# A convolution's tap matrices split ahead of time and a second channel tile on VectorE in a four-layer encoder kernel

## The chip, the cores and the metric

The kernel runs on one core of one Trainium2 chip. A core has a TensorE for matmuls (PE; its weight loads are shown as PEld), a VectorE (DVE), a ScalarE (ACT), a GpSimd engine (POOL) and a SyncE (SP) that issues most DMAs; ACT and POOL issue some too. Each engine works through its own queue in order; waits between engines are semaphores that a library sets from the data dependences. The metric is the device time of the whole program in microseconds (us). Data lie in SBUF (128 partitions) and PSUM (eight banks of 128 x 512 floats, which TensorE writes).

## The reference

The input is x of 512 tokens by 1024 channels in float32. Four layers follow; each adds a token mixer and then a channel mixer to x:

```python
for i in range(DEPTH):                     # 4
    mixer, j = i % N_MIXERS, i // N_MIXERS
    h = rmsnorm(x, norm1_g[i])
    if mixer == 0:   y = conv_module(h, ...)      # layers 0 and 3
    elif mixer == 1: y = nat_mixer(h, ...)        # layer 1
    else:            y = retention_mixer(h, ...)  # layer 2
    x = x + y
    x = x + conv_ffn(rmsnorm(x, norm2_g[i]), ...)

def conv_module(h, w_in, b_in, dw_w, dw_b, ln_g, ln_b, w_out):
    a, gt = jnp.split(h @ w_in + b_in, 2, axis=-1)
    u = a * jax.nn.sigmoid(gt)
    u = dwconv(u, dw_w, dw_b)              # 31 taps over the tokens, each channel by itself
    u = layernorm(u, ln_g, ln_b)
    return jax.nn.silu(u) @ w_out
```

The change is in the two uses of `conv_module` (layers 0 and 3, j = 0 and 1) and in the channel mixers `conv_ffn` of layers 0, 1 and 2.

## The kernel before

**Precision.** Every float32 operand of a matmul is split in two parts: a high part, cast by ScalarE to the reduced format fp32r, and a low part, the difference, made by VectorE. Three matmuls replace one: high by high, high by low, low by high (`mm3`, L161 to L164, for most; L483 to L485 for the taps). A weight tile (`load_w`, L154 to L159) is loaded on SP into one of two `wraw` buffers, cast into one of three `whi` buffers (L157) and subtracted into one of three `wlo` buffers (L158). `split` (L171 to L173) does the same for other tiles.

**Stages.** `ffn(l, after)` is a channel mixer: 44 up projections `up(n)` of 24 matmuls each, in pairs (value and gate), each pair followed by `mid` on VectorE and ScalarE; then eight output tiles of 66 matmuls. `conv(j, after)` is the convolution module.

**A convolution.** The 1024 channels are eight tiles m of 128. `front(m)` makes the two input projections of a tile (48 matmuls of 128 x 512) and from them u = a * sigmoid(g). Seven tiles take the TensorE path: u is copied by eight small GpSimd DMAs (L435) to `xf`, in which a partition holds a channel and a phase of time, and split into `X`. `taps(m, X, half)` then runs the 31 taps as matmuls against tap matrices, in four units per tile, two per half. A unit is one 128 x 1216 piece of `cdw`: loaded on SP into `raw` (608 KB, five buffers, L473), split into `W` (high and low, three buffers), and used by 2 groups x 5 slots x 3 = 30 small matmuls (64 x 128 or 64 x 112 outputs). A half ends with VectorE adding the bias into `y` (L494), and at set points with `bn_stats` (L502) for the layer norm over channels; the table `BNG` says which units' channels are counted together and after which unit.

Tile 6 (`CD`) takes the VectorE path: `direct` runs its 31 taps as 31 `scalar_tensor_tensor` over 128 x 512 (L446; the last, L454, in two halves that also reorder), `CTAPS` of them in each step of the loop, and at the end four transposes on TensorE (L460) and a copy on ScalarE put the result into `y`. The statistics of the RMS norm are made in between: `stats1` (sums, four transposes, a chain of small VectorE operations to `rstd_col`) and `stats2` (four transposes that broadcast it, L209).

The loop that orders this is L511 to L519: step n emits `front` of the n-th tile of `CORDER` (6, 0, 1, 2, 3, 4, 5, 7), then some direct taps, then the second half of the taps of the tile two back, then the first half of the tile one back. After the last taps, 13 matmuls on old data (L507) fill the time of the layer norm's statistics.

**What sets the order.** Inside the `TileContext` a planner simulates the program, emits instructions to each engine's queue when they are ready in its own clock, with the order in the source as priority, and gives out buffers. `tc.high_priority` (`hp()`) raises a priority; `tc.issue_after(i)` (through `behind(name)`) holds back what is traced in its block until instruction i stands ahead of it on the same engine. A stage's pools may reuse the memory of the stage before, tile by tile. In the first convolution (`early`) the first weights are loaded at the start of the program and some order is written by hand.

## Time and profile before

| | us |
|---|---|
| median of three runs | 2578.81 (2578.18 to 2578.84) |
| the profiled execution, device time | 2577.98 |
| its span in the trace | 2576.2 |
| TensorE busy | 2558.8 |
| VectorE, ScalarE, GpSimd busy | 1652.3, 1050.0, 258.8 |
| bytes moved by DMA | 271.78 MB, 105 GB/s on average |

The stages follow one another: the first convolution until about 205 us, its channel mixer until 590, the neighbourhood attention until 830, the next mixer until 1200, the retention until 1630, the third mixer until 2001.6, the second convolution until 2201, the last mixer until the end. A row of the timeline gives start, duration, engine, line and operation, output and inputs, shape and count; the bracket behind it says how long the engine was idle before it and what ended that. Matmuls are pipelined: their rows overlap, so the distance between starts is their price. A few matmul records are missing from the trace.

### The profile page before, as it was taken

Reading aid. Unit: us, or ns where it says so; the run is one execution under the profiler, and the core shown is the slowest. Engines: PE = TensorE matmul, PEld = TensorE weight load, DVE = VectorE, ACT = ScalarE, POOL = GpSimd, SP = SyncE. Lnnn points to the kernel's source line nnn. Section 1 sums busy time; section 2 is a strip of 40 time slices with the busy share of each in tenths; the row PEclk is TensorE's granted clock in tenths of the full one; section 3 lists DMA queues with packets and bytes.
Section 4 is the critical chain, followed back from the end, with each engine's and each line's share of the span. In section 5 each row is a group of like instructions: output and inputs, shape, how many; then the busy total and the mean of one; then the engine's idle time right before and its main releaser. Section 6 shows DMA issues by size and latency. Waiting matters only on the chain.

```text
span 2576.2 us, 33719 instructions
## 1 busy us (share of the span) xinstructions
PE 2558.8 (99%) x13414; PEld 2120.2 (82%) x13414; DVE 1652.3 (64%) x2673; ACT 1050.0 (41%) x1439; POOL 258.8 (10%) x301
## 2 busy tenths in 40 slices
PE   9999999999999999999999999999999999999999
PEld 7878888889998888888888888888888888788888
DVE  7986777338877777624656566677743787677732
ACT  5554444335556444423333323444432445444421
POOL 1213000003421100000000000100000221100000
PEclk9999999999999999999999999999999999999999
DMA  6724232333332322233222221232333672222232
GB/s 241 234 86 148 90 98 88 95 103 105 97 91 71 101 95 95 90 97 110 74 85 71 84 80 58 98 99 90 97 90 97 206 222 74 90 93 95 92 107 80
DMA packets 80174, 271.78 MB, mean 105 GB/s; under 512 B 10720, under 2 KB 13664, under 8 KB 80016
## 3 DMA queue, kind: packets, MB, share of 16 engines
q1 hardware_dynamic: 73152, 256.32, 30.9%
q0 software_dynamic: 5568, 10.59, 1.7%
q10 hardware_dynamic: 1296, 2.72, 0.3%
q8 instruction: 105, 1.72, 0.3%
q14 instruction: 53, 0.43, 0.1%
HBM read 260.19 MB, written 5.63 MB: 103 GB/s over the span
## 4 chain that ended last, share of the span: by engine, by line
PE 97%; DVE 2%; ACT 0%; issue 0%; DMA 0%; SPq 0%; DVEq 0%; ACTq 0%
PE ps L164 27%; PE ps L163 27%; PE ps L162 27%; PE ps L168 3%; PE ps L169 3%; PE ps L167 3%; PE ps L485 1%; PE ps L484 1%; PE ps L483 1%; PE ps L332 1%; PE ps L333 1%; PE ps L337 1%; PE ps L724 1%; DMA x<-in_xT 0%; PE ps L539 0%
## 5 line engine op out<-in xcount | busy, mean ns | idle before, releaser
L157 ACT CAST wh<-wr 128x1024 fp32r<-128x1024 f32 (+1 forms) x410 | 423.1, 1033 | 1086.1 <-PE ps L163 775.9
L164 PE MATMUL ps<-xh,wl 128*128 128x512 f32 x1856 | 735.4, 397 | 0.1
L163 PE MATMUL ps<-xl,wh 128*128 128x512 f32 x1856 | 734.5, 396 | 0.2 <-DVE xl L232 0.2
L162 PE MATMUL ps<-xh,wh 128*128 128x512 f32 x1856 | 730.4, 394 | 0.4 <-ACT wh L157 0.4
L158 DVE TENSOR_TENSOR wl<-wr,wh 128x1024 fp32r<-128x1024 f32 (+1 forms) x407 | 494.9, 1216 | 334.4 <-ACT wh L157 332.1
L162 PEld LDWEIGHTS ps<-xh,wh 128*128 128x128 f32 x1856 | 348.5, 188 | 85.8 <-ACT wh L157 1.3
L163 PEld LDWEIGHTS ps<-xl,wh 128*128 128x128 f32 x1856 | 348.4, 188 | 85.9 <-DVE xl L232 0.5
L164 PEld LDWEIGHTS ps<-xh,wl 128*128 128x128 f32 x1856 | 348.3, 188 | 81.7 <-DVE wl L158 0.5
L162 PE MATMUL ps<-hh,wh 128*128 128x512 f32 (+1 forms) x726 | 281.6, 388 | 0.5 <-DVE x L362 0.5
L163 PE MATMUL ps<-hl,wh 128*128 128x512 f32 (+1 forms) x726 | 281.5, 388 | 0.0
L164 PE MATMUL ps<-hh,wl 128*128 128x512 f32 (+1 forms) x726 | 281.5, 388 | 0.0
L298 DVE TENSOR_TENSOR t<-ps,rstd_bc 128x512 f32<-128x512 f32 x176 | 120.8, 690 | 159.1 <-PE ps L164 159.1
L250 POOL TENSOR_TENSOR sqacc<-t,sqacc 128x512 f32<-128x512 f32 x49 | 75.1, 1533 | 1253.6 <-ACT t L245 1248.2
L162 PEld LDWEIGHTS ps<-hh,wh 128*128 128x128 f32 x726 | 136.6, 188 | 31.0 <-DVE x L362 0.7
L163 PEld LDWEIGHTS ps<-hl,wh 128*128 128x128 f32 x726 | 136.7, 188 | 30.3
L164 PEld LDWEIGHTS ps<-hh,wl 128*128 128x128 f32 x726 | 136.7, 188 | 30.3
L168 PE MATMUL ps<-wl,xh 128*128 128x256 f32 (+1 forms) x512 | 159.1, 312 | 0.5 <-DVE wl L158 0.5
L169 PE MATMUL ps<-wh,xl 128*128 128x256 f32 (+1 forms) x512 | 159.1, 312 | 0.0
L167 PE MATMUL ps<-wh,xh 128*128 128x256 f32 (+1 forms) x512 | 158.4, 312 | 0.0
L301 ACT ACTIVATE t<-t,par 128x512 f32<-128x512 f32 x176 | 142.5, 814 | 6.0 <-DVE t L298 5.8
L305 DVE SCALAR_TENSOR_TENSOR t<-t,par,t 128x511 f32<-128x511 f32 x176 | 132.0, 750 | 5.5
L303 DVE SCALAR_TENSOR_TENSOR t<-t,par,t 128x511 f32<-128x511 f32 x176 | 130.8, 744 | 0.0
(256 smaller groups left out, 3572.4 us busy)
## 6 DMA issues: line engine op xcount, KB each, us to landing
wr<-in_f_up SPq DMA_DIRECT2D x176, 512.0 KB, 3.4
wraw<-in_cdw SPq DMA_DIRECT2D x56, 608.0 KB, 5.1
wr<-in_f_down SPq DMA_DIRECT2D x64, 448.0 KB, 3.3
wr<-in_f_down SPq DMA_DIRECT2D x32, 512.0 KB, 3.5
wr<-in_cw_in SPq DMA_DIRECT2D x30, 512.0 KB, 3.9
wr<-in_nat_qkv SPq DMA_DIRECT2D x24, 512.0 KB, 3.5
wr<-in_cw_out SPq DMA_DIRECT2D x16, 512.0 KB, 3.9
wr<-in_ret_qk SPq DMA_DIRECT2D x16, 512.0 KB, 3.5
```

The source lines that it names most:

```text
L157: nc.scalar.copy(hi[:, :n], raw[:, :n])
L158: eng.tensor_tensor(lo[:, :n], raw[:, :n], hi[:, :n].bitcast(F32), SUB)
L162: nc.tensor.matmul(o, wh, ah, start=first, stop=False)
L163: nc.tensor.matmul(o, wh, al, start=False, stop=False)
L164: nc.tensor.matmul(o, wl, ah, start=False, stop=last)
L167: nc.tensor.matmul(o, ah, wh, start=first, stop=False)
L168: nc.tensor.matmul(o, ah, wl, start=False, stop=False)
L169: nc.tensor.matmul(o, al, wh, start=False, stop=last)
L298: nc.vector.tensor_tensor(u, ps, rstd_bc, MUL)
L301: nc.scalar.activation(a, u, AF.Identity, bias=pc("fdb", l * 44 + c), scale=pt[:, w + 1:w + 2])
L303: nc.vector.scalar_tensor_tensor(a[:, 1:], u[:, :T - 1], pt[:, w:w + 1], a[:, 1:], MUL, ADD)
L305: nc.vector.scalar_tensor_tensor(a[:, :T - 1], u[:, 1:], pt[:, w + 2:w + 3], a[:, :T - 1], MUL, ADD)
```

## The change

Three things are changed.

1. The tap matrices of the second convolution's remaining 24 units (`UNITS`) are split during the channel mixers of layers 0, 1 and 2: at the odd n from 5 to 35 of each, `split_taps` loads half a unit, splits it and stores both parts to a tile in HBM (`wsp`). 3 x 16 halves are 24 units. The second convolution loads the finished pair (128 x 2 x 1216) straight into `W`, which has five buffers there, and makes no split.
2. In the second convolution tile 5 joins tile 6 on the VectorE path: `CDS` lists the tiles, the order is 6, 5, 0, 1, 2, 3, 4, 7, the direct taps come up to 10 in a step, and the first taps on TensorE start one step later. One group of `bn_stats` is taken at a later unit there.
3. Order, in both convolutions: the direct taps are emitted behind the taps of their step and end a step earlier; the transposes of a direct tile (`direct_out`) are held behind the latest tap matmul. In the first convolution the splits of `W` for a first half are held behind the tile's `X`. In the second the front of a tile is held behind the taps ahead of it. The RMS statistics get the high priority, and some weight loads and matmuls near them are held behind `rstd_col` or the broadcast transposes.

```diff
-BNG = ((0, 16, 16), (16, 28, 24), (28, 30, 30), (30, 31, 31), (31, 32, 32))
+BNG = (((0, 16, 16), (16, 28, 24), (28, 30, 30), (30, 31, 31), (31, 32, 32)),
+       ((0, 16, 16), (16, 28, 30), (28, 30, 30), (30, 31, 31), (31, 32, 32)))
-CORDER = (CD, 0, 1, 2, 3, 4, 5, 7)
-CTAPS = (0, 3, 5, 5, 5, 5, 5, 3, 0, 0)
+CDS = ((6,), (6, 5))
+CORDER = ((6, 0, 1, 2, 3, 4, 5, 7), (6, 5, 0, 1, 2, 3, 4, 7))
+CTAPS = ((0, 4, 5, 5, 6, 6, 5, 0, 0, 0), (0, 5, 10, 10, 10, 9, 9, 9, 0, 0))
+UNITS = [m * 4 + b for m in CORDER[1][2:] for b in range(4)]
...
     def ffn(l, after):
+            sp = st.enter_context(tc.tile_pool(name=nm("sp"), bufs=1, reuse_waits=RW))
+            def split_taps():
+                unit, g = state["units"].pop(0)
+                c = slice(g * GW, (g + 1) * GW)
+                raw = sp.tile([P, GW], F32, tag="raw", name=nm("spr"))
+                nc.sync.dma_start(raw, cdw[1, unit][:, c])
+                w = sp.tile([P, 2, GW], F32R, tag="w", name=nm("spw"))
+                split(raw, w[:, 0], w[:, 1])
+                nc.gpsimd.dma_start(wsp[unit][:, :, c], w.bitcast(F32))
...
                 if n > 1:
                     ups.append(up(n))
+                if n % 2 and 5 <= n <= 35 and l < DEPTH - 1:
+                    split_taps()
...
-                def front(m):
+                def front(m, n):
+                    nd = len(CDS[j])
...
-                        stats1()
-                        stats2(rph)
+                        with hp():
+                            stats1()
+                            stats2(rph)
                     else:
                         for (ps, c) in ((pg, m + 8), (pa, m)):
-                            wh, wl = load_w(cw_in[j, c], D)
+                            pin = m == CORDER[j][1] and c == (m if early else m + 8)
+                            with behind("col") if c == m == CORDER[j][2 if early else 1] else ExitStack():
+                                wh, wl = load_w(cw_in[j, c], D)
                             for k in range(KD):
                                 s = slice(k * P, (k + 1) * P)
-                                mm3(ps, wh[:, s], wl[:, s], xhi[k], xlo[k], k == 0, k == KD - 1)
+                                held = j and c == m + 8 and k == 0 and n > nd + 1
+                                with behind("tap") if held else behind("bc") if pin and k == (6 if early else 1) or early and m + 8 == c == CORDER[j][2] + 8 and k == 0 else ExitStack():
+                                    mm3(ps, wh[:, s], wl[:, s], xhi[k], xlo[k], k == 0, k == KD - 1)
...
+                def direct_out(m):
+                    with behind("tap"):
+                        ps, yr = bank(psb), state["yr"]
                         for r in range(SH):
                             nc.tensor.transpose(ps[:, r * P:(r + 1) * P], yr[:, r * P:(r + 1) * P], ident)
-                        nc.scalar.copy(y[:, :, CD * P:(CD + 1) * P],
-                                       ps.rearrange("p (r c) -> p r c", r=SH))
+                        nc.scalar.copy(y[:, :, m * P:(m + 1) * P], ps.rearrange("p (r c) -> p r c", r=SH))
...
                 def taps(m, X, half):
+                    X, state["xc"], state["xl"] = X
...
-                        raw = dp.tile([P, 2 * GW], F32, tag="wraw", name=nm("wraw"), bufs=5)
-                        if early and m * 4 + b < 5:
-                            after_squares(raw[:, :1])
-                        nc.sync.dma_start(raw, cdw[j, m * 4 + b])
-                        W = dp.tile([P, 2, 2 * GW], F32R, tag="W", name=nm("W"), bufs=3)
-                        with tc.issue_after(state["u"].ins) if early and m * 4 + b < 5 else ExitStack():
-                            split(raw, W[:, 0], W[:, 1])
+                        W = dp.tile([P, 2, 2 * GW], F32R, tag="W", name=nm("W"), bufs=5 if j else 3)
+                        if j:
+                            nc.sync.dma_start(W.bitcast(F32), wsp[m * 4 + b])
+                        else:
+                            raw = dp.tile([P, 2 * GW], F32, tag="wraw", name=nm("wraw"), bufs=5)
+                            if early and m * 4 + b < 5:
+                                after_squares(raw[:, :1])
+                            nc.sync.dma_start(raw, cdw[j, m * 4 + b])
+                            with behind(*(("u", "rph") if early and m * 4 + b < 5 else ("xc", "xl")[:2 - 2 * half])):
+                                split(raw, W[:, 0], W[:, 1])
...
                 for n in range(10):
+                    order, nd = CORDER[j], len(CDS[j])
                     if n < 8:
-                        fr[n] = front(CORDER[n])
-                    direct(done, done + CTAPS[n])
-                    done += CTAPS[n]
-                    if n >= 3:
-                        taps(CORDER[n - 2], fr[n - 2], 1)
-                    if 2 <= n <= 8:
-                        taps(CORDER[n - 1], fr[n - 1], 0)
+                        fr[n] = front(order[n], n)
+                    if n >= nd + 2:
+                        taps(order[n - 2], fr[n - 2], 1)
+                    if nd < n <= 8:
+                        taps(order[n - 1], fr[n - 1], 0)
+                    direct(done, done + CTAPS[j][n])
+                    done += CTAPS[j][n]
+                    if n in (4, 7)[2 - nd:]:
+                        direct_out(CDS[j][-1] if n == 7 else CDS[j][0])
...
+    wsd = ctx.enter_context(tc.tile_pool(name="wsd", bufs=1, space=bass.MemoryType.DRAM))
+    wsp = {u: wsd.tile([P, 2, 2 * GW], F32, tag=f"ws{u}", name=nm("ws")) for u in UNITS}
+    state["units"] = [(u, g) for u in UNITS for g in range(2)]
```

`direct` now counts through the taps of all tiles of `CDS[j]` in turn, and `direct_end` holds the last tap, unchanged. `state["tap"]` is the latest tap matmul, `state["col"]` the copy to `rstd_col`, `state["bc"]` the latest broadcast transpose, `state["xc"]` and `state["xl"]` the cast and the low part of a tile's X. The table of parameters gains one tile's tap weights.

More of the change, by code (lines that the diff above doesn't have):

```diff
@@ L208, in bcast @@
         for b in range(4):
-            nc.tensor.transpose(
+            state["bc"] = nc.tensor.transpose(
                 ps[:, b * P:(b + 1) * P], col[:, b:b + 1].broadcast_to([P, P]), ident)
@@ L257, in stats1 @@
         r = rsqrt(v, 4)
-        nc.vector.tensor_copy(rstd_col, r)
+        state["col"] = nc.vector.tensor_copy(rstd_col, r)
     def stats2(phased=None):
@@ L264, in stats2 @@
         if phased is not None:
[L265 removed]
+            state["rph"] = nc.scalar.copy(phased, ps.rearrange("p (q s) -> p s q", s=PH))
     def residual(k, ps, perm=False):
@@ L378, in conv @@
                 nc.scalar.dma_start(bias, cdb[j])
-            bst = cp.tile([P, SH, len(BNG), 6], F32, tag="bst", name=nm("bst"))
+            bst = cp.tile([P, SH, len(BNG[j]), 6], F32, tag="bst", name=nm("bst"))
             rph = cp.tile([P, PH, NQ], F32, tag="rph", name=nm("rph"))
@@ L384, in conv @@
                 us = [up.tile([P, PH, QL], F32, tag=f"u{i}", name=nm("u")) for i in range(2)]
-                ud = up.tile([P, T + CW - 1], F32, tag="ud", name=nm("ud"))
-                yd = up.tile([P, T], F32, tag="yd", name=nm("yd"))
-                nc.vector.memset(ud[:, :CW // 2], 0.0)
-                nc.vector.memset(ud[:, T + CW // 2:], 0.0)
+                uds, yds = {}, {}
+                for m in CDS[j]:
+                    uds[m] = ud = up.tile([P, T + CW - 1], F32, tag=f"ud{m}", name=nm("ud"))
+                    yds[m] = up.tile([P, T], F32, tag=f"yd{m}", name=nm("yd"))
+                    nc.vector.memset(ud[:, :CW // 2], 0.0)
+                    nc.vector.memset(ud[:, T + CW // 2:], 0.0)
                 for u in us:
@@ L436, in front, with direct @@
                     X = dp.tile([P, PH, 2, QL], F32R, tag="X", name=nm("X"), bufs=3)
-                    split(xf, X[:, :, 0, :], X[:, :, 1, :])
-                    return X
-                def direct(k0, k1):
-                    for k in range(k0, k1):
-                        w = pc("cwd", j * CW + k)
+                    state["xl"] = split(xf, X[:, :, 0, :], X[:, :, 1, :])
+                    state["xc"] = state["cast"]
+                    return X, state["xc"], state["xl"]
+                def direct(n0, n1):
+                    for n in range(n0, n1):
+                        m, k = CDS[j][n // CW], n % CW
+                        i = j + n // CW
+                        ud, yd = uds[m], yds[m]
+                        w = pc("cwd", i * CW + k)
                         if k == 0:
-                            nc.vector.tensor_scalar(yd, ud[:, :T], w, pc("cbd", j), MUL, ADD)
+                            nc.vector.tensor_scalar(yd, ud[:, :T], w, pc("cbd", i), MUL, ADD)
                         elif k < CW - 1:
@@ L485, in taps @@
                                 mm = nc.tensor.matmul(o, xg[:, 1, q], W[:, 0, w], start=False, stop=a == 3)
+                    state["tap"] = mm
                     c0 = m * P + half * 64
@@ L498, in taps @@
                         c1 = m * 4 + half * 2 + b.stop
-                        for n, (a0, a1, at) in enumerate(BNG):
+                        for n, (a0, a1, at) in enumerate(BNG[j]):
                             if c1 == at:
@@ L1132, in _layout @@
     put("fdb", cols(f["ffn_dw_b"]))
-    cd = slice(CD * P, (CD + 1) * P)
-    put("cwd", f["conv_dw_w"][:, :, cd].transpose(2, 0, 1).reshape(P, -1))
-    put("cbd", f["conv_dw_b"][:, cd].T)
+    cds = [(j, slice(m * P, (m + 1) * P)) for j in range(2) for m in CDS[j]]
+    put("cwd", np.concatenate([f["conv_dw_w"][j, :, c].T for j, c in cds], 1))
+    put("cbd", np.stack([f["conv_dw_b"][j, c] for j, c in cds], 1))
     half = 128
```

30 lines of the change are left out of this document (15 added, 15 removed).

## The prediction

> **What bounds the kernel now.** The page first: its first two parts and the engine line of the chain that ended last.
>
> ```profile
> span 2576.2 us, 33719 instructions
> ...
> PE 2558.8 (99%) x13414; PEld 2120.2 (82%) x13414; DVE 1652.3 (64%) x2673; ACT 1050.0 (41%) x1439; POOL 258.8 (10%) x301
> ...
> PEclk9999999999999999999999999999999999999999
> ...
> PE 97%; DVE 2%; ACT 0%; issue 0%; DMA 0%; SPq 0%; DVEq 0%; ACTq 0%
> ```
>
> TensorE works through the whole span at full clock, so the end moves only by TensorE work removed and by its idle time gained or lost. Next the busy time by stage (columns: stretch, length, busy time and count of PE, PEld, DVE, ACT, POOL, granted clock, DMA share, GB/s), here the first channel mixer:
>
> ```profile
> 205.00:590.00 385.00, 385.00 (x1711) 312.19 (x1710) 231.32 (x296) 152.15 (x179) 31.50 (x41) 1.00 0.33 105
> ```
>
> No idle there; the idle time lies in the two convolutions. The timeline of PE in the second one (start, duration, line, operation) gives all the prices:
>
> ```profile
> 2001.57 0.40 PE L162 MATMUL ps<-xh,wh 128*128 128x512 f32 x1
> ...
> 2117.68 0.39 PE L162 MATMUL ps<-xh,wh 128*128 128x512 f32 x1
> ...
> 2124.45 0.40 PE L164 MATMUL ps<-xh,wl 128*128 128x512 f32 x1
> 2126.76 0.63 PE L460 MATMUL ps<-ident,t 128*128 128x128 f32 x4 [1.92 <-DVE t L454]
> 2127.15 0.30 PE L483 MATMUL ps<-W,X 128*64 128x128 f32 x1
> ...
> 2127.41 0.21 PE L483 MATMUL ps<-W,X 128*64 128x112 f32 x1
> ...
> 2129.19 0.21 PE L483 MATMUL ps<-W,X 128*64 128x112 f32 x1
> ...
> 2137.90 0.22 PE L485 MATMUL ps<-W,X 128*64 128x128 f32 x1
> ...
> 2140.63 0.28 PE L485 MATMUL ps<-W,X 128*64 128x128 f32 x1 [0.94 <-DVE X L173]
> ...
> 2147.64 3.17 PE L507 MATMUL ps<-xh 128*128 128x512 f32 x13
> ```
>
> Between 2117.68 and 2124.45 lie 29 steps of front: 0.2334 us each, so a front of 48 takes 11.2 us. Between 2127.41 and 2129.19 lies one unit of taps (30 matmuls): 1.78 us. A group of four transposes costs about 0.44. I call E the end of the last front: 2124.45 + 0.23 = 2124.68. Check: 384 front matmuls, 18 units and two groups from the statistics make 89.6 + 32.0 + 0.9 = 122.5 of the 123.1 us from 2001.57 to E. The last tap ends at 2147.64, E + 22.96, though ten units and a group are only 18.3. The rest is idle: 2126.76 - E = 2.1 for the last VectorE tap (L454), and some 2.5 between 2137.90 and 2140.63, where X of tile 7 is late. The first convolution has the same shape:
>
> ```profile
> 130.68 0.40 PE L164 MATMUL ps<-xh,wl 128*128 128x512 f32 x1
> 133.00 0.63 PE L460 MATMUL ps<-ident,t 128*128 128x128 f32 x4 [1.93 <-DVE t L454]
> ...
> 153.85 3.17 PE L507 MATMUL ps<-xh 128*128 128x512 f32 x13
> ```
>
> E is 130.91 here, the last tap ends at E + 22.94, the idle is 2.1 + 2.5 again.
>
> **The second convolution up to E.** Tile 5 leaves TensorE: 4 units x 1.78 = 7.14 us. Its result needs one more group of transposes, and tile 6's group moves ahead of E (tile 5's now stands behind it): +0.44. So E falls by 6.7.
>
> The first taps now follow the front of tile 0 after one front only, and the next front is held behind them (`behind("tap")`), so X of tile 0 must be ready 11.2 us after its own front. The chain of tile 7, from the DVE, POOL and ACT timelines and the answer for xf:
>
> ```profile
> 2126.46 0.73 DVE L431 SCALAR_TENSOR_TENSOR u<-t,par,t 128x512 f32<-128x512 f32 x1
> ...
> 2127.49 4.16 POOL L435 DMA_DIRECT2D xf<-u  x8 [15.06 <-DVE u L431]
> ...
> DMA to landing us min/median/max: 2.0/2.6/3.8
> ...
> 2137.49 0.64 ACT L172 CAST X<-xf 128x544 fp32r<-128x544 f32 x1
> ...
> 2139.84 0.73 DVE L173 TENSOR_TENSOR X<-xf,X 128x544 fp32r<-128x544 f32 x1
> ```
>
> From E to the last issue 2131.65 - 2124.68 = 7.0, then 2.6 to 3.8 landing, 0.64 cast, 0.73 low part: 10.9 to 12.2 us against 11.2. The wait is 0 to 1, with slower copies up to 3; it cannot be below nothing. I take 0.5, since three of four ends of that chain lie within 1 us of 11.2. E becomes 2118.5.
>
> **The second convolution after E.** Ten units stand behind E as before, now tiles 3, 4 and 7. The late VectorE tap goes (tile 5's taps are done behind the taps of tile 4), and ACT and DVE no longer split anything:
>
> ```profile
> L173 DVE TENSOR_TENSOR W<-wraw,W 128x1216 fp32r<-128x1216 f32 x56 | 79.1, 1422 | 9.2 <-ACT W L172 8.5
> L172 ACT CAST W<-wraw 128x1216 fp32r<-128x1216 f32 x56 | 67.9, 1212 | 56.8 <-PE ps L485 53.9 <-DMA wraw<-in_cdw 2.4 <-DVE sm L179 0.3
> L446 DVE SCALAR_TENSOR_TENSOR yd<-ud,par,yd 128x512 f32<-128x512 f32 x58 | 43.3, 747 | 0.6
> ```
>
> DVE loses 28 x 1.42 = 40 us of splits and gains 31 x 0.75 = 23 us of taps: relief, worth nothing by itself, since DVE was not late elsewhere. X of tile 7 no longer queues behind casts, and would be there about E + 11 to 12, when PE has done six units and a group (11.1). By PE and X alone the last tap would end at E + 18.3 to 19.3.
>
> But what is late next is the transfer. One unit's raw taps were 608 KB; the split pair is twice that, 1.245 MB, and five buffers hold 14 to 18 when E comes. The loads of 19 to 23 start when 14 to 18 are released.
>
> ```profile
> 2010.00:2015.00 5.00, 5.00 (x23) 4.04 (x22) 3.81 (x12) 0.53 (x2) 0.00 (x0) 1.00 1.02 414
> 104.00:108.00 4.00, 4.00 (x48) 3.62 (x47) 4.00 (x5) 1.45 (x3) 0.17 (x1) 1.00 1.01 326
> 2060.00:2065.00 5.00, 5.00 (x57) 4.54 (x55) 4.32 (x6) 3.37 (x3) 1.38 (x3) 1.00 0.93 275
> ...
> wraw<-in_cdw SPq DMA_DIRECT2D x56, 608.0 KB, 5.1
> wr<-in_f_up SPq DMA_DIRECT2D x176, 512.0 KB, 3.4
> ...
> q0 software_dynamic: 256, 0.28, 7.0%
> ```
>
> Full engines move 414 GB/s when large rows alone are in flight; about 326 and 275 beside the small copies to xf. At 414 a pair takes 3.0 us, more than the 1.78 PE needs for it. The fixed part of a load is 3.4 - 0.524 MB / 414 = 2.1. The copies to xf took 7.0% of 20 us = 1.4 (the row is that of the 20 us around E), and one load of output weights 1.3. So the last tap ends at E + 1.8 (unit 14) + 2.1 + 5 x 3.0 + 1.4 + 1.3 + 1.8 (unit 23) = E + 23.4. That is 2118.5 + 23.4 = 2141.9 against 2147.64: **-5.7**. Ends: -9.8 (hidden, E + 19.3 = 2137.8) and the slow rates below. I take the full rate because these loads have rows of 9.7 KB and the small copies are priced apart.
>
> The Trainium skill's page "DMA: Bandwidth & Descriptors", section "Where 436 GB/s comes from", speaks against the change: HBM would feed one core at about 358 GB/s, not more. The row above disagrees for its 5 us. By the page (an estimate) the last tap would end 2.4 us later, and the whole sum would be -4.6.
>
> Between E's of successive fronts the loads fit: four pairs, two weights and the copies need 12.0 + 2.5 + 1.4 = 16 us of 18.3. The statistics' group over tiles 4 to 6 moves to tile 7, but its inputs are ready earlier and DVE is idle then: nothing; if it ran late, four bn_stats, 2 us.
>
> **The first convolution.** No unit goes; the waits change. Rows around its E:
>
> ```profile
> 131.72 1.14 DVE L454 SCALAR_TENSOR_TENSOR t<-ud,par,yd 128x256 f32<-128x256 f32 x2
> 132.69 1.22 DVE L158 TENSOR_TENSOR wl<-wr,wh 128x1024 fp32r<-128x1024 f32 x1
> 133.82 0.74 DVE L431 SCALAR_TENSOR_TENSOR u<-t,par,t 128x512 f32<-128x512 f32 x1
> ...
> 143.72 0.64 ACT L172 CAST X<-xf 128x544 fp32r<-128x544 f32 x1
> ...
> 146.06 0.73 DVE L173 TENSOR_TENSOR X<-xf,X 128x544 fp32r<-128x544 f32 x1
> ```
>
> All 31 taps are now done a front earlier and the transposes stand behind taps, so the 2.1 us wait goes. X of tile 7 is late next: its u loses L454 from its path (0.97) and perhaps L158 (1.13), so its cast can begin 1.0 to 2.1 earlier. Tile 7's first two splits are now queued behind X on ACT and DVE; behind those wait only the remaining W splits, for which PE waits: X cast 0.64, W cast 1.2, W low part 1.4 let the second matmul start 3.3 us after that cast begins; now X's low part ends 146.79 - 143.72 = 3.1 us after it, no earlier. So the gain is 1.0 to 2.1, less what three taps (2.2 us) moved into a full DVE stretch (4.00 of 4.00 in the row at 104) push back: I take **-1.3**; ends -4.6 (both waits gone) and +1.
>
> **The channel mixers.** Each of three gains 16 split_taps: a 304 KB load on SP, half a W split on ACT and DVE, a 608 KB store issued by POOL. At most 16 x 1.21 on ACT (152 busy of 385) and 16 x 1.42 on DVE (231). The cover: three wh buffers.
>
> ```profile
> L157 ACT CAST wh<-wr 128x1024 fp32r<-128x1024 f32 x346 | 362.7, 1050 | 851.0 <-PE ps L163 544.9 <-issue 205.9 <-PE ps L169 49.9
> ```
>
> ACT's casts wait for PE, not the reverse; each is made two weight tiles, 2 x 5.6 us, ahead. A split that blocks ACT (one raw and one w buffer, so it waits for the last store) costs nothing below about 11 us, and one comes every 11.2. A store should land in 5 to 8 (the 608 KB load took 5.1). SP and POOL pay an issue each; POOL is busy 31.5 of 385. Traffic rises from 105 GB/s by 45 MB over three mixers, some 40 GB/s. I count 0; with the cover gone, 1 us a split would be +48.
>
> **Sum.** -5.7 - 1.3 = -7.0 on the profiled run, 2577.98 (span 2576.2 and 1.8 around it): 2571.0. The median of the runs, 2578.81, is 0.8 higher, so I say **2571.8**.
>
> **Rivals.**
> 1. The loads hide: E + 19.3, so -9.8 - 1.3 = -11.1, 2567.7. For it: SP may issue the output weights elsewhere. Against: five pairs at any rate seen exceed PE's need.
> 2. The mixed rate, 326, holds: 7.0 MB (five pairs, copies, one weight) take 21.6 us, the tail ends at E + 1.8 + 2.1 + 21.6 + 1.8 = E + 27.3, so -1.8 - 1.3 = -3.1, 2575.7: no measurable change. The rate that the Trainium skill's page "DMA: Bandwidth & Descriptors" gives lies between this one and the forecast's.
> 3. Slower: the loads bound the whole stretch. From unit 0's release (about 2049.6) 19 pairs, nine weights and five copies, 29.8 MB, must land: 2049.6 + 2.1 + 1.8 + 29.8 MB / rate. At 275 that is 108.4 us and the last tap ends at 2161.9, +14.3 - 1.3 = +13, 2591.8. It decides below about 310 GB/s, exceeds +0.2% below 296. Against: rows of 9.7 KB, and weights come in 4 KB rows at 414.
> 4. The change doesn't do what it says: the planner sets another order, and a pinned instruction (the held fronts, the splits behind X) makes PE wait for what was removed. 3 us at tile 0, 1 in the first convolution and rival 2's tail: -6.7 + 3 + 4.3 + 1 = about +2, 2580.4.
>
> **How the numbers follow.** 0.2% is 5.2 us, about what a measurement of this kernel can tell from no change. Chances: forecast (-5.2 to -9) 0.45, rival 1 0.18, rival 2 0.18, rival 3 0.08, rival 4 0.11. Faster 0.63, same 0.29, slower 0.08. The range 2565.5 to 2579.5 takes in the forecast, rivals 1 and 2 and the nearer half of 4; left out are rival 3, the rest of 4 and both far ends together.
>
> **What would show it.** 720 tap matmuls instead of 840 in the second convolution; E 6 to 7 us earlier after its start; no wait of the transposes on the last VectorE tap; gaps before units 20 to 23 ended by the loads of W, some 5 us in all; mixers still without PE idle. PE waiting before the first taps, or the DMA share at 1 long before E, would make it wrong; so would ACT stalled in a mixer by a store.

## The result, and the profile after

The changed kernel is slower: 2597.85 us, median of 4 runs (2595.53 to 2598.92), against 2578.82 (2578.18 to 2580.84) beside it. The ratio is 1.0069, with a 95% interval of 1.0057 to 1.0081; the forecast was 2571.8, its range 2565.5 to 2579.5. The profiled execution took 2597.8, its span 2596.0.

From the page of the changed kernel: the busy times and the new DMAs (their KB, and the median us from issue to landing):

```profile
PE 2560.5 (99%) x13298; PEld 2120.9 (82%) x13298; DVE 1671.5 (64%) x2722; ACT 1046.0 (40%) x1459; POOL 288.1 (11%) x341
...
ws<-spw POOLq DMA_DIRECT2D x48, 608.0 KB, 4.3
W<-ws SPq DMA_DIRECT2D x24, 1216.0 KB, 10.2
```

PE has 116 fewer matmuls (13414 - 13298: four units of 30 gone, four transposes added), yet its busy time is 1.7 us longer, so matmuls that were left ran slower. Where the time went is read from the timeline of PE at the same marks in both kernels: the first of the 13 filling matmuls behind a convolution's last tap (L507 before, L544 after), the first matmul of a mixer (L332, L346), and the first and the last front of the second convolution. Rows of the kernel before that were not shown yet:

```profile
206.52 0.39 PE L332 MATMUL ps<-xh,wh 128*128 128x512 f32 x1
829.22 0.40 PE L332 MATMUL ps<-xh,wh 128*128 128x512 f32 x1
1631.57 0.40 PE L332 MATMUL ps<-xh,wh 128*128 128x512 f32 x1
2201.37 0.47 PE L332 MATMUL ps<-xh,wh 128*128 128x512 f32 x1 [0.88 <-DVE x L554]
```

And of the changed kernel:

```profile
156.73 0.45 PE L544 MATMUL ps<-xh 128*128 128x512 f32 x1
214.32 0.39 PE L346 MATMUL ps<-xh,wh 128*128 128x512 f32 x1
837.02 0.40 PE L346 MATMUL ps<-xh,wh 128*128 128x512 f32 x1
1640.66 0.40 PE L346 MATMUL ps<-xh,wh 128*128 128x512 f32 x1
2012.91 0.40 PE L165 MATMUL ps<-xh,wh 128*128 128x512 f32 x1
2137.44 0.40 PE L167 MATMUL ps<-xh,wl 128*128 128x512 f32 x1
2167.46 0.91 PE L544 MATMUL ps<-xh 128*128 128x512 f32 x3
2221.19 0.47 PE L346 MATMUL ps<-xh,wh 128*128 128x512 f32 x1 [0.87 <-DVE x L594]
```

The differences of neighbouring marks, in us (E is the end of the last front, 0.23 behind its last matmul's start; "forecast" is the step of the prediction):

| stretch | before | after | gained or lost | forecast |
|---|---|---|---|---|
| first convolution to its last tap | 153.85 | 156.73 | +2.9 | -1.3 |
| its output projection | 52.67 | 57.59 | +4.9 | 0 |
| first mixer, attention | 622.70 | 622.70 | 0 | 0 |
| second mixer, retention | 802.35 | 803.64 | +1.3 | 0 |
| third mixer | 370.00 | 372.25 | +2.2 | 0 |
| second convolution to E | 123.11 | 124.76 | +1.7 | -6.2 |
| from E to its last tap | 22.96 | 29.79 | +6.8 | +0.4 |
| its output projection | 53.73 | 53.73 | 0 | 0 |
| last mixer | 374.83 | 374.81 | 0 | 0 |

The sum is +19.8. The list of PE's waits (in all, times, longest, us) names what PE waited for in the changed kernel:

```profile
PE ps L521 <- DVE X L176: 5.9, 3, 2.9
PE ps L519 <- DMA W<-ws: 5.4, 1, 5.4
PE ps L212 <- DVE rstd_col L261: 3.7, 3, 1.6
PE ps L519 <- ACT X L175: 3.5, 2, 1.8
```

The busy time by stretch has what waits alone don't show (stretch, length, busy time of PE, PEld, DVE, ACT, POOL, granted clock, DMA share, GB/s); for comparison, every row of the kernel before in the prediction has the clock at 1.00:

```profile
2060.00:2065.00 5.00, 1.51 (x14) 1.36 (x15) 5.00 (x8) 0.54 (x1) 1.80 (x4) 0.59 0.42 117
...
2150.00:2155.00 5.00, 0.98 (x13) 0.70 (x11) 3.39 (x7) 3.06 (x4) 0.00 (x0) 0.81 1.02 420
2155.00:2160.00 5.00, 1.88 (x18) 1.91 (x19) 0.00 (x0) 0.00 (x0) 0.00 (x0) 0.50 0.82 340
2160.00:2165.00 5.00, 5.00 (x62) 5.00 (x61) 0.78 (x2) 0.00 (x0) 0.00 (x0) 0.67 0.02 5
```

Around four groups of waits the granted clock is at half (around the waits for `rstd_col` it is not). By the trace's record of the clock it was so for 27.3 us inside the kernel: 6.8 in the first convolution, 3.4 behind it, 6.8 and 10.2 in the second; in the profiled execution of the kernel before, for none.

So three questions for the experiments: what the 8.4 us outside the fronts and taps of the convolutions are (the output projection and two mixers), why the second convolution waits, and what the clock adds.

### The profile page after: what moved, and what is told of

It reads as the page before. It is cut to its first block, busy times and chain, and to the rows that moved or that the text cites. A ratio compares the mean times of both kernels' runs of the same rounds, so it can differ in the third digit from the quotient of the medians.

```text
span 2596.0 us, 33769 instructions
## 1 busy us (share of the span) xinstructions
PE 2560.5 (99%) x13298; PEld 2120.9 (82%) x13298; DVE 1671.5 (64%) x2722; ACT 1046.0 (40%) x1459; POOL 288.1 (11%) x341
## 4 chain that ended last, share of the span: by engine, by line
PE 90%; DVE 4%; issue 3%; DMA 2%; ACT 1%; POOL 1%; SPq 0%; DVEq 0%; ACTq 0%; POOLq 0%
PE ps L165 26%; PE ps L167 26%; PE ps L166 26%; PE ps L171 3%; PE ps L172 3%; PE ps L170 3%; DMA ws<-spw 1%; PE ps L521 1%; PE ps L519 1%; PE ps L520 1%; DVE wl L161 1%; DVE yd L475 1%; PE ps L764 1%; POOL sqacc L253 0%; DVE xl L235 0%
## 6 DMA issues: line engine op xcount, KB each, us to landing
W<-ws SPq DMA_DIRECT2D x24, 1216.0 KB, 10.2
```

## The experiments

Theory A: the 48 splits do not stay beside the fronts where the source has them. They wait for nothing but their own load, so the planner issues them early, into stages whose VectorE and ScalarE work PE waits for. Theory B: in the second convolution a chain to X lost its cover, and PE's own order waits for loads too early; transfers as such are not the bound. Theory C: a wait of PE also costs the clock behind it. Rivals: the prediction's steps (splits cost nothing; loads bound the end), and its third rival (loads bound the whole second convolution).

Ratios below are to the kernel before, run beside each, with the 95% interval.

**1. The splits alone**, in the kernel before; nobody reads what they store.

```diff
 # before.py
+            def split_taps(): ...            # as in the change
...
+                if n % 2 and 5 <= n <= 35 and l < DEPTH - 1:
+                    split_taps()
```

> The kernel before with nothing but the 48 half-unit splits added to the first three channel mixers (the stored low and high parts are read by nobody, both convolutions are those of before). The prediction's step 'the splits hide behind the mixers' gives 2578.8 us, within 1 us. The theory 'splits get pulled in front of other stages' vector and scalar work, since they wait for nothing but their load' gives the output projection of the first convolution about 3 to 5 us longer and the waits ahead of the second and third mixer's first matmul about 1 to 2 us longer each: 2584 to 2587 us, with PE gaps at the row broadcast of the statistics.

2590.84 us, ratio 1.0044 (1.0028 to 1.0061), above even the 2584 to 2587 of the theory: more than half of the loss comes from the splits without either convolution being changed. ScalarE's timeline in the changed kernel shows them in the output projection of the first convolution, between the layer norm's work (yn, sh), each behind the store of the split before it, since there is one buffer `w`:

```profile
158.90 0.69 ACT L175 CAST spw<-spr 128x608 fp32r<-128x608 f32 x1
...
165.16 0.70 ACT L175 CAST spw<-spr 128x608 fp32r<-128x608 f32 x1 [1.04 <-DMA ws<-spw]
165.77 0.61 ACT L175 CAST sh<-yn 128x512 fp32r<-128x512 f32 x1
```

While ScalarE waits for a store, the `sh` behind it, which PE needs, waits too (1.6 us in PE's waits, none before). VectorE takes a low part into the middle of the chain for the norm's statistics:

```profile
159.61 0.79 DVE L176 TENSOR_TENSOR spw<-spr,spw 128x608 fp32r<-128x608 f32 x1
160.32 0.15 DVE L200 SCALAR_TENSOR_TENSOR sm<-sm,sm 128x4 f32<-128x4 f32 x1
```

In the second and third mixer it is the same with the RMS statistics: PE's row broadcast waits for `rstd_col`, 1.6 us at most. The run has one more loss, 1.7 us in the first convolution, where nothing differs in the waits. There the rows of this run, and then of the kernel before, are:

```profile
133.00:137.00 4.00, 3.79 (x34) 3.82 (x35) 1.78 (x3) 0.59 (x1) 1.35 (x3) 0.57 0.42 129
```

```profile
133.00:137.00 4.00, 4.00 (x64) 4.00 (x65) 1.83 (x3) 1.80 (x2) 1.56 (x4) 1.00 0.41 140
```

After the same wait of 1.9 us one execution kept its clock and did 64 matmuls in 4 us, the other did 34 at a mean clock of 0.57. So the same wait cost 0 or 1.7 us more. Of the eight profiles with this order of the first convolution (the kernel before and runs 1, 9, 10, 11 and 12), five have 3.4 us at half clock in it and three have none.

**2. The splits held** where the source puts them.

```diff
 # after.py
+        state["wd"] = nc.sync.dma_start(raw[:, :n], src)      # load_raw
...
+        state["wc"] = nc.scalar.copy(hi[:, :n], raw[:, :n])   # split_w
+        lw = eng.tensor_tensor(lo[:, :n], raw[:, :n], hi[:, :n].bitcast(F32), SUB)
+        if eng is nc.vector: state["wv"] = lw
...
-                    split_taps()
+                    with behind("wd", "wc", "wv"):
+                        split_taps()
```

> The changed kernel with every split of a half unit held, on the queues of SyncE, ScalarE and VectorE, behind the weight load and the weight split of the front beside which the source puts it; nothing else moves. If the splits cost time because they are pulled in front of other stages' work, as the run with the splits alone suggests (+11 us there), the output projection of the first convolution is 5 us shorter, the waits ahead of the second and third mixer 1 to 2 us shorter each: 2588 to 2591 us, the second convolution unchanged. If they cost time by their mere work on ScalarE and VectorE or by their stores, they cost it wherever they stand: 2595 to 2600 us.

2587.61 us, 1.0031 (1.0019 to 1.0044), just below the range expected. The output projection is back at its old length:

```profile
155.98 0.45 PE L547 MATMUL ps<-xh 128*128 128x512 f32 x1
...
208.71 0.39 PE L348 MATMUL ps<-xh,wh 128*128 128x512 f32 x1
```

52.73 us, and no wait for `rstd_col` is left in the list. The second mixer and the retention take 801.80 us there, and 801.81 in run 10, which has no splits at all. So the splits themselves are hidden, as the prediction said, when they are done in the mixers; what cost 8 to 10 us was where they were done. Theory A holds.

**3. Half the loads**, and **4. splits in place**. The first loads W's low part once for all units (the other units' low parts are left out); the second has no splits in the mixers and splits the raw taps in the second convolution as the kernel before did, with four raw buffers.

```diff
 # 3
-                            nc.sync.dma_start(W.bitcast(F32), wsp[m * 4 + b])
+                            nc.sync.dma_start(W0.bitcast(F32), wsp[m * 4 + b][:, 0])
+                            W1 = state["W1"]
 # 4
-                if n % 2 and 5 <= n <= 35 and l < DEPTH - 1:
+                if False:
...
-                            nc.sync.dma_start(W.bitcast(F32), wsp[m * 4 + b])
+                            nc.sync.dma_start(raw, cdw[j, m * 4 + b])
+                            split(raw, W[:, 0], W[:, 1])
```

> The changed kernel with W's low part of the second convolution loaded once and used for all units (this leaves out the other units' low parts), so W's loads move half the bytes, while PE, VectorE, ScalarE and the order stay. If the transfers bound the second convolution (the wait for W of 5.4 us at its end, and the late copies of x behind it), it gives back about 5 us at the end and 2 to 6 us at the X waits: 2586 to 2592 us. If the second convolution's gaps come from the in-order queues and from the clock at half after a wait of PE, less than 2 us at the X waits goes, and the wait for X of the first tile (5 us, clock at half behind it) stays as it is.

> The changed kernel with no splits in the mixers: the second convolution loads the raw taps and splits them in place as the kernel before did, but has both channel tiles on VectorE. If the early splits cost 8 us up to the second convolution, its first matmul comes 8 us earlier. In the second convolution VectorE then has about 24 x 1.9 us of splits' low parts more than the changed kernel. If VectorE's load decides there, the second convolution gets longer by 5 to 15 us and the total is 2592 to 2605 us; if the transfers alone decided, it gets shorter by 5 us and the total is 2583 to 2587 us.

Half the loads: 2592.73 us, 1.0049 (1.0034 to 1.0064), just outside what was expected for a transfer bound. The wait for W shrank from 5.4 to 1.5 us (0.42 and 1.04), but X of tile 7 was waited for 4.1 us in its place, and the first X as before, 4.9 us. Splits in place: 2582.22 us, 1.0009 (1.0000 to 1.0018), faster than either side expected. VectorE had all its splits back in the second convolution, and PE waited 3.6 us there for splits of W (1.24, 1.39, 0.21 and 0.75), so VectorE's load costs less than the 5 to 15 us expected of it. The first X was still waited for 4.9 us, with half the bytes in flight, and in the changed kernel the copies to its `xf` landed 2.1 us after their issue at the median. So the loads do not make that wait. Its chain in the changed kernel, by the timelines of VectorE and ScalarE:

```profile
2048.02 0.69 DVE L450 TENSOR_TENSOR t<-ps,rph 128x512 f32<-128x512 f32 x1 [0.30 <-issue]
2048.63 1.41 DVE L475 SCALAR_TENSOR_TENSOR yd<-ud,par,yd 128x512 f32<-128x512 f32 x2
2049.95 1.22 DVE L161 TENSOR_TENSOR wl<-wr,wh 128x1024 fp32r<-128x1024 f32 x1
2051.08 0.75 DVE L456 SCALAR_TENSOR_TENSOR u<-t,par,t 128x512 f32<-128x512 f32 x1
...
2063.19 0.72 DVE L176 TENSOR_TENSOR X<-xf,X 128x544 fp32r<-128x544 f32 x1
```

```profile
2059.90 0.64 ACT L175 CAST X<-xf 128x544 fp32r<-128x544 f32 x1 [0.25 <-DMA xf<-u]
```

Tile 0's front ended at about 2047.4 (the next front's end, 2058.6, less 48 x 0.2334). Two direct taps and a weight's low part stand between `t` and `u` in VectorE's order, and X's low part starts 2.65 us behind the end of its cast, behind direct taps, a weight's low part and the next tile's `u`. The chain takes 16.5 us to 2063.91; one front covers 11.2.

**5. Tile 0's front before tile 5's**, so that two fronts cover that chain.

```diff
-CORDER = (..., (6, 5, 0, 1, 2, 3, 4, 7))
+CORDER = (..., (6, 0, 5, 1, 2, 3, 4, 7))
+CTILES = ((0, 1, 2, 3, 4, 5, 7), (0, 1, 2, 3, 4, 7))    # the order of the taps, as it was
```

> The changed kernel with the second convolution's fronts in the order 6, 0, 5, 1, 2, 3, 4, 7 in place of 6, 5, 0, 1, 2, 3, 4, 7: the chain from tile 0's front to its X has two fronts of matmuls as cover (22 us) in place of one (11 us). If the 4.7 us of wait for X and the half clock behind it (6.8 us at half, worth at most 3.4 us) come from that short cover, both go: 2590 to 2594 us, and the wait for W at the end stays. If the transfers bound the second convolution (the rival that the prediction priced at 2591.8 us), what is gained at the start is lost at the end, where W comes as late as before: 2596 to 2599 us.

2591.0 us, 1.0046 (1.0032 to 1.0060). The first taps follow the front without a gap:

```profile
2058.53 0.22 PE L520 MATMUL ps<-W,X 128*64 128x128 f32 x1
```

What was gained at the start was kept, so the third rival (loads bound the whole stretch) falls; the wait for W of 5.4 us at the end stayed.

**6. Matmuls to fill that last wait.** 20 of them, behind the first unit of tile 7.

```diff
+                        if j and m == 7 and half == 0 and i == 1:
+                            wf = bank(psa)
+                            with tc.issue_after(mm.ins):
+                                for _ in range(20):
+                                    state["fill"] = nc.tensor.matmul(wf, xhi[0][:, :P], xhi[0], start=True, stop=True)
```

> The changed kernel with 20 matmuls of 128x512 on nothing needed, queued ahead of the unit whose W came 5.4 us late at the end of the second convolution. 20 x 0.215 us fill 4.3 us of that wait. If a wait of PE of this length costs more than itself, since the granted clock is at half for 10.2 us behind it, the units behind it run at full clock: 3 to 5 us faster, 2593 to 2595 us. If the clock costs nothing there (the rest is bound by W's loads), the time stays within 1 us of the changed kernel or is some tenths longer.

2603.86 us, 1.0093 (1.0079 to 1.0107): slower, against the expectation. The filler did not stand in the wait but behind it:

```profile
2157.25 0.34 PE L525 MATMUL ps<-W,X 128*64 128x128 f32 x1 [5.44 <-DMA W<-ws]
...
2160.48 6.10 PE L517 MATMUL ps<-xh 128*128 128x512 f32 x20
```

That is how the cause of the wait came to light. The wait is not between the first and the second unit, but two matmuls into the first. PE's order in the changed kernel reads there, with the numbers of the buffers (W3203 is the first of tile 7's four units, W3207 the third; L521 is the matmul that needs X's low part). The numbers are from the program's list of instructions; the trace has the same lines in the same order, without them:

```
L519 MATMUL ps3202<-W3203,X3190 64x128
L520 MATMUL ps3202<-W3203,X3190 64x128
L519 MATMUL ps3205<-W3207,X3190 64x128
L520 MATMUL ps3205<-W3207,X3190 64x128
L521 MATMUL ps3202<-W3203,X3190 64x128
```

The planner put two matmuls of the third unit ahead of the one that needs X's low part; presumably PE was idle there in its clock and that W loaded, but its clock is not shown here. On the chip that W was not loaded, and PE, which works in order, waited for it with two units' work behind.

**7. The last two units in order**, and **8. the filler ahead of the wait**, behind tile 4's last unit (26 matmuls, in PE's order ahead of all of tile 7's).

```diff
 # 7
+                                with behind("tap") if j and last else ExitStack():
                                     nc.tensor.matmul(o, xg[:, 0, q], W[:, 0, w], start=a == 1, stop=False)
```

> The changed kernel with the matmuls of the last two units held behind those of the two before them; nothing else. In the changed kernel's PE order the first two matmuls of the third of the last four units stand behind the first two of the first of them, where the planner took PE to be idle for X's low part, and PE, which works in its order, waits there 5.4 us for that unit's W while the two units before it have all they need. If this order is what costs, and not the rate of the loads, the wait for W goes but for at most 1 us, the wait for X's low part (some 1.6 us) stands in its place, and the half clock behind it gets shorter: 2592 to 2594 us. If the loads bound the end, W of the last two units is waited for in the new place and the time stays within 1 us of the changed kernel.

> The changed kernel with 26 matmuls of 128x512 on nothing needed, this time ahead of the wait itself: behind the last unit of tile 4 and ahead of the first matmul that waits for tile 7's X, so PE works 26 x 0.215 = 5.6 us of the 7.1 us in which it waited. If the clock falls for a wait and not for what PE does afterwards, the four units behind it take 7.1 us at full clock in place of 9.3 us: about 2 us faster than the changed kernel, 2595 to 2596.5 us, although PE has 5.6 us more to do. If the granted clock does not hang on the wait, the time is that of the changed kernel or longer.

In order: 2595.7 us, 1.0059 (1.0045 to 1.0072), less of a gain than expected, and with four runs not clear of the changed kernel's 2597.85; run 12 repeats the step with eleven. First the changed kernel, then the run in order:

```profile
2152.36 0.27 PE L519 MATMUL ps<-W,X 128*64 128x128 f32 x1 [1.70 <-ACT X L175]
2152.47 0.22 PE L520 MATMUL ps<-W,X 128*64 128x128 f32 x1
2158.12 0.34 PE L519 MATMUL ps<-W,X 128*64 128x128 f32 x1 [5.43 <-DMA W<-ws]
```

```profile
2152.20 0.27 PE L520 MATMUL ps<-W,X 128*64 128x128 f32 x1 [1.57 <-ACT X L175]
2154.23 0.37 PE L522 MATMUL ps<-W,X 128*64 128x128 f32 x1 [1.70 <-DVE X L176]
...
2162.74 3.18 PE L545 MATMUL ps<-xh 128*128 128x512 f32 x13
```

With E at 2137.64 the last tap ends at E + 25.1 in place of E + 29.8, and no wait for W is left at all, with the same bytes. So in the two profiles the order costs 4.7 us. But the loads are only just out of the way. In the changed kernel the last five were issued and landed so:

```profile
L505 SPq DMA_DIRECT2D W<-ws x5: 319/319/320, 2139.5 to 2148.9; - x5
...
DMA to landing us min/median/max: 5.7/10.2/12.0
```

The last one is the slowest: it landed at 2160.9, E + 23.2. In the run in order it landed at 2160.6, and its unit started at 2160.9, 0.3 us later. (In the row of the changed kernel from 2160 above the DMA share is 0.02: the bytes were moved by then, but the load counts as landed only at 2160.9.) X of tile 7 was late beside these loads too: its copies to `xf` landed 5.1 to 7.8 us after their issue in the changed kernel, against 2.0 to 3.8 in the kernel before. So Theory B holds for the first X and for PE's order; but once the order is mended the transfers are the next bound, 0.3 us away.

With the filler ahead: 2594.21 us, 1.0056 (1.0042 to 1.0070), a little faster than expected.

```profile
2153.84 6.12 PE L504 MATMUL ps<-xh 128*128 128x512 f32 x26
...
2161.26 0.25 PE L525 MATMUL ps<-W,X 128*64 128x128 f32 x1 [1.19 <-DMA W<-ws]
...
2168.30 0.44 PE L550 MATMUL ps<-xh 128*128 128x512 f32 x1
```

The four units behind the wait took 2168.30 - 2161.26 = 7.0 us, in the changed kernel 2167.46 - 2158.12 = 9.3: the clock's price is 2.3 us there, and 6.1 us of useless work (26 matmuls, 0.23 apart) bought it back. The granted clock is 1.00 in this run's rows from 2150 to 2168. The profiled execution was the slowest of the four (2597.54; the others took 2594.1 to 2594.3) and lost time in other stages, so it is these rows that show Theory C, more than the median.

**9. The first convolution's order as before**, all else as changed (no pins, tap counts 3, 5, 5, ..., taps of VectorE ahead of PE's).

> The changed kernel, with the first convolution's order of work (pins, tap counts per front, tap chain ahead of the taps) as before. If the new order of the first convolution is what lost 2.9 us there, this run takes 2594 to 2596 us and the first convolution's last tap ends about 3 us earlier; the output projection after it stays 5 us longer, since the splits are still in it. The prediction, which gave the new order a gain of 1.3 us, would have this run 1.3 us slower than the changed kernel.

2597.11 us, 1.0068 (1.0053 to 1.0083): 0.7 us faster than the changed kernel, where the theory expected 2 to 4 and the prediction 1.3 slower. Such runs don't resolve 0.7 us, and this one left the question open.

**10. The second tile alone**, and **11. all mended.** The first is run 4 with run 5's order and the first convolution as before; a second one adds run 7's pin. "All mended" is runs 2, 5, 7 and 9 together, with the stored matrices.

> The second channel tile on VectorE without the stored tap matrices: second convolution splits its raw taps in place, the first convolution's order is as before, fronts of the second in the order 6, 0, 5, 1, 2, 3, 4, 7. If the 7.1 us of matmuls that tile 5 no longer needs are worth their time as soon as no wait takes it back, this takes 2571 to 2575 us, faster than both kernels. If VectorE's load (two tiles' taps beside the splits) is a bound of its own in the second convolution, it stays at 2578 to 2583 us.

> The run with the second tile alone (taps split in place, tile 0's front before tile 5's, the first convolution as before), with the last two units held behind the two before them. There was no wait for W there, so the theory of the planner's order gives no more than the 0.4 to 1 us by which the X waits near the end may shrink: 2573.5 to 2575.5 us, faster than the kernel before by 0.1 to 0.25%.

> The stored tap matrices with all that the runs so far mended: splits held in the mixers, tile 0's front before tile 5's, the last units in order, the first convolution's order as before. From the single steps: 2597.9 less 10.2 (held), 6.9 (tile 0 earlier), 4 to 5 (last units) and 0.7 (first convolution) is 2575 to 2576 us. If stored matrices spare VectorE and ScalarE something that is worth time in the second convolution, this beats the run with the second tile alone (2574.9 us); if not, it is the same or up to 3 us slower, since it loads twice as much.

| run | us | ratio (95%) |
|---|---|---|
| second tile alone | 2574.86 | 0.9981 (0.9972 to 0.9990) |
| with the pin | 2575.28 | 0.9984 (0.9975 to 0.9993) |
| all mended, stored matrices | 2575.73 | 0.9981 (0.9972 to 0.9990) |

All three beat both kernels, by 4 to 5 us against the kernel before. Stored matrices gain nothing over splitting in place, and cost 48 loads and 48 stores. In the profiles of the first and the third row they gain 1.6 us up to E (117.5 against 119.1 from the first front) and lose 2.9 behind it (25.2 against 22.4), where twice the bytes are loaded. The marks of the mended run:

```profile
2001.62 0.39 PE L168 MATMUL ps<-xh,wh 128*128 128x512 f32 x1
...
2118.92 0.40 PE L170 MATMUL ps<-xh,wl 128*128 128x512 f32 x1
...
2144.37 0.44 PE L548 MATMUL ps<-xh 128*128 128x512 f32 x1
```

E is 117.5 us behind the first front; the prediction said 116.9. That is 5.6 us less than before, and 0.85 of the rest is a wait for X that is left, so the price of tile 5's four units (6.7) was about right.

**12. One step taken out of the mended kernel.** With eleven runs each, smaller steps show. Once the new order of the first convolution is put back, once the pin on the last units is taken out, and the mended kernel runs again beside them.

> The mended kernel with stored tap matrices (held splits, tile 0's front before tile 5's, last units in order), but with the first convolution in the changed kernel's new order. If that order costs what the profiles show (its first convolution ends 1.2 us later on the mean of eight profiles against six, with the clock at half for 6.8 us in place of 0 to 3.4), this is 1 to 3 us slower than the mended kernel's 2575.7: 2576.5 to 2579 us. By the prediction's step (a gain of 1.3 us) it is 2574 to 2575 us.

> The mended kernel with stored tap matrices, but without the pin that holds the last two units behind the two before them; PE's order then has again two matmuls of the third of the last four units between the first and the second slot of the first. If that order costs a wait for a load that nothing else needs so early, this is 4 to 6 us slower than the mended kernel: 2579.5 to 2582 us, with a wait for W of about 5 us near the end. If it is no more than a place in which an unavoidable wait shows, the time is within 1 us of 2575.7.

> The mended kernel with stored tap matrices once more, beside the two runs that take one step out of it: 2574.5 to 2577 us, so that the differences are taken on one chip.

2577.4 (2574.89 to 2578.88), 2578.83 (2578.28 to 2580.19) and 2575.79 us (2573.51 to 2578.65), 11 runs each. By the medians the new order of the first convolution costs 1.6 us, and the order of the last units 3.0, less than the 4 to 6 expected. The median with the new order, and every run without the pin, lie above ten of the eleven runs of the mended kernel beside them. Without the pin the wait is back as it was:

```profile
2138.97 0.34 PE L522 MATMUL ps<-W,X 128*64 128x128 f32 x1 [5.45 <-DMA W<-ws]
```

Behind the first convolution's waits, first with the new order, then in the mended run:

```profile
147.00:155.00 8.00, 7.88 (x97) 7.88 (x98) 5.80 (x12) 3.00 (x4) 0.00 (x0) 0.70 0.00 0
```

```profile
147.00:155.00 8.00, 7.00 (x114) 6.86 (x115) 7.79 (x19) 4.03 (x6) 0.00 (x0) 1.00 0.01 2
```

Ahead of this PE idles 4.3 us with the new order (1.24, 1.94 and 1.12) and 3.8 without (1.93, 0.91 and 0.92), nearly the same; but the new order has put it in one place, 142.2 to 147.1, and the clock is at half around it for 6.8 us: 97 matmuls in the 8 us behind it where it was 114. The mended run is not free of this: its record of the clock has 3.4 us at half behind the wait of 1.93, from 132.9. What fills the block in the new order, VectorE's timeline shows in the changed kernel:

```profile
143.18 1.94 DVE L539 BATCH_NORM_STATS2 bst<-y 128x6 f32<-128x384 f32 x4
145.03 0.71 DVE L176 TENSOR_TENSOR X<-xf,X 128x544 fp32r<-128x544 f32 x1
```

X's cast began there at 141.0, 2.7 us earlier than in the kernel before. But X's low part stood behind four `bn_stats`, and the first low part of W, pinned behind it, ended at 147.1, when PE could go on.

## Why the prediction was wrong

The steps lie 26.8 us above the forecast for the profiled execution (2597.8 against 2571.0): 8.4 from the splits, 4.2 in the first convolution, 14.2 in the second.

- **The channel mixers: "I count 0".** This step failed. The prediction found cover in the mixers (three `wh` buffers), and held splits are free there (run 2). But it took the source's place for the place on the queues. The planner emits what is ready, and the splits wait for one load only, so they were ready in earlier stages. "One raw and one w buffer, so it waits for the last store" was said, and priced for ScalarE's weight casts only, not for `sh` and the statistics. The loss, 8.4 us by the marks and 10.2 between the medians of the changed kernel and run 2, belongs to no rival.
- **The first X: "The wait is 0 to 1, with slower copies up to 3", taken as 0.5.** Wrong size: 4.7 us, and half clock behind it. The chain's durations came from tile 7 in the kernel before, where VectorE had few direct taps left. In the changed kernel the taps come ten to a step and stand in the same order as `u` and X's low part. "Relief, worth nothing by itself" counted VectorE's total and not what stands ahead of what. With this wait, 1.5 us for a later tile's X (at 2122.9) and the clock, E came 124.8 us behind the first front, not 116.9.
- **"But what is late next is the transfer", with the last tap at E + 23.4.** The transfer was mis-sized a little, and PE's order was not thought of. The full rate was there, 420 GB/s in the row from 2150 to 2155, but not throughout (325 from 2140 to 2150, 340 from 2155 to 2160): the last load landed at E + 23.2, between the forecast's E + 21.6 and rival 2's E + 25.5. The Trainium skill's page "DMA: Bandwidth & Descriptors", section "Where 436 GB/s comes from", has 358 GB/s from HBM for one core; the row of 420 disagrees for its 5 us. By the loads alone the last tap would end about E + 25 (an estimate, the last landing and one unit of 1.8). It ended at E + 29.8, and the rest, some 4.7 us with what the clock added, came from PE's order: the wait of 5.4 us that looked like the forecast's was for a unit that was not next (run 7). X, for which the prediction had E + 18.3 to 19.3, is as late as the loads: in run 7 PE waits for X of tiles 4 and 7 three times (1.57, 1.57 and 1.70 us), with half clock from the last of them on, and the tail still ends at E + 25.1, 0.3 us behind what the last load allows. So that the loads no longer show as a wait there is in part luck.
- **The first convolution, "-1.3".** Wrong sign: +1.6 by run 12, +2.9 in the profiled pair. The pair overstates it, since the kernel before had no half clock there and five of the eight profiles with its order have 3.4 us. The transposes' wait of 2.1 went, as said, and X's cast came 2.7 us earlier, more than the 1.0 to 2.1 forecast. What failed is the price of what follows that cast: the prediction had 3.3 us from its start to the second matmul, and it was 6.1 (141.0 to 147.1), since X's low part waited behind four `bn_stats` and the splits of W were pinned behind X. (In the second convolution four `bn_stats` stood ahead of that low part too, from 2151.64; the prediction had put that group at nothing.) PE's idle time came together in one block, and the clock paid.
- **"TensorE works through the whole span at full clock, so the end moves only by TensorE work removed and by its idle time gained or lost."** True of the profile of before, and then used as if the clock could not move. No step or rival had a price for it. In the profiled execution it is about 2.3 us at the last units and about 1.9 at the first (from 2063.96 to 2067.7 at half, 3.7 us for 1.9 of work), and some 4.5 more in and behind the first convolution (an estimate from the record of the clock: 6.8 and 3.4 us at half, of which PE worked 9.1). These are parts of the losses above, not added to them.
- **Removed work.** About right: of the 6.7 us that tile 5's units are worth net, the mended kernel gains 5.6 up to E, and 4 to 5 in all.
- **The rivals.** Rival 3 gave 2591.8, nearest to the result, but by luck: its mechanism, loads that bound the whole stretch, was not there (runs 4, 5 and 7). Rival 4, that the planner sets another order and PE waits for what was removed, was the right kind, with 0.11 and 2580.4, and it had a wait of 3 us for tile 0's X (4.7 was measured). But it looked at pins alone, while the splits in the mixers and the order of the last units, some 15 of the 26.8 us, were not pinned.

## What to carry to other kernels

Work that depends on nothing but its own load has no place of its own: under a planner it moves to the first idle moment of its engines, so hold it on each of its queues, or count it in the earliest stage that it can reach. Time a chain by what will stand between its steps in the changed kernel, not by a row of the old one. And when a wait is ended by a load, look which instruction waits and what is ready behind it, before the load is taken to be late; and when the wait is gone, look how long before its use the load landed.

## What the runs showed of the hardware

- A wait of PE can cost more than itself. In the changed kernel the clock was at half for 27.3 us, in pieces of 3.4, 6.8 and 10.2 us. The Trainium skill's page "TensorE: Matmul & The Clock Gate", section "What's actually happening", has a window of about 3.4 us, after an idle one of which the clock falls to half; the lengths agree. A whole idle window was not needed: a wait of 1.9 us was enough in run 1, and not in the kernel before. At half clock the 128x512 matmuls of run 6 started 0.43 us apart, at full clock 0.23.
- Half clock costs only what PE does in it: the last 10.2 us at half cost 2.3, since PE stood still for nearly half of it.
- The eight small copies to `xf` land later under the loads of W: 6.7 us at the median for tile 7 in the changed kernel against 2.6 before, 7.9 in run 3 with half of W's bytes, and 5.1 in run 10 with half the bytes and the splits in place, so it is not the bytes alone. What does it was not tried.
